# Turned outputs issued piece by piece, the inverse's fourth product one step later, and two sets of key factors put in by ScalarE

## The chip, the cores and the metric

The kernel runs on one core of one Trainium2 chip. The core has five engines with instruction queues of their own: TensorE (PE in the profile, its weight loads PEld), VectorE (DVE), ScalarE (ACT), GpSimd (POOL) and SyncE (SP). SP only issues transfers here; ScalarE's queue issues transfers too, between its arithmetic. The metric is the device time of one execution in microseconds (us), as the median of several runs. The kernel before takes 2236.08 us, the median of three runs from 2230.81 to 2239.41.

## What is computed

One layer of a decoder: a normalised input (512 tokens of 2048) is projected once, and the columns of the projection feed two causal token mixers, their gates and two merge gates. The mLSTM has 8 heads, the gated DeltaNet 16. Their outputs go through one output projection, are merged with sigmoid gates and added to the input; a last RMSNorm ends it. Cut to what matters here:

```python
u = rmsnorm(x, norm_w)
(ml_q, ml_k, ml_v, ml_o, ml_z, ml_i, ml_f,
 dn_qkv, dn_z, dn_b, dn_a, gate_a, gate_b) = split(u @ w_in)

# mLSTM, per head and chunk
kw = k_c * exp(we_c - m_new)[..., None]
C_new = decay * C + einsum('sd,se->de', kw, v_c)

# gated DeltaNet, per head and chunk
a_mat = where(strict, beta[..., :, None] * (k @ k.T) * decay_mat, 0.0)
sol = triangular_solve(a_mat + eye, rhs, lower=True, unit_diagonal=True)
u_ = w_val - w_k @ S
o = q_dec @ S + qk @ u_
S_new = g_end * S + k_end.T @ u_

y = sigmoid(gate_a) * (h_a @ w_out[:2048]) + sigmoid(gate_b) * (h_b @ w_out[2048:])
out = rmsnorm(x + y) * final_norm_w
```

## The kernel before

**Products in fp32 from two halves.** Each weight tile (wr) is loaded by SP, and then split: ScalarE rounds it to a high part wh (L135), VectorE subtracts to get the low part wl (L138). Three products for each pair of tiles (wh by uh, wh by ul, wl by uh: L261 to L263) give nearly the exact fp32 product. Weights are loaded four blocks ahead (RAHEAD) and split three blocks ahead (SAHEAD).

**The stages.** First the input is normalised, then come the projections that need no channel-major layout, in a Strassen-like scheme of seven products for eight (`seven_stage`, L575 to L577). Then comes the stage of the mixers: eight units (`dn_unit`), one for two DeltaNet heads each, numbered 0 to 7 here. A unit projects its keys, in units 3 to 6 the query and key of one mLSTM head too, then its values and queries (`proj_cm`). After that come the output projection and the end.

**What sets the order.** The order on TensorE is the order of the code. A projection calls `tick()` after every six products: that is a step. All other work of the mixers is written as generators, and each `yield n` hands the engine back for n steps. So the small products of the mixers stand between the projection's products at places that the yields fix. On the other engines a scheduler sets the order, from priorities (`urgent`) and from `behind(eng)`, which places an instruction after the newest split on that engine. An engine then runs its queue strictly in that order, so an instruction that waits holds all behind it.

**The parts around the change:**

- `turn` (L790 to L797) transposes a tile of a head in 32x32 blocks on VectorE. `travel` (L799 to L812) then finishes the transpose through DRAM, with four transfers (L806) of 64 KB each. Keys, values and queries go by SP's queue, to a buffer td and back (L811). Outputs go by ScalarE's queue to h_d (DeltaNet) or hm_d (mLSTM) and are read only in the output projection. An output's `travel` starts `lag` steps after its transpose: five, and three for the heads of the last unit.
- `dn_front_k` (L814) makes the triangular matrix of a unit. The products of keys by keys (pk, L841) are taken with the decay into aq (L843), the factors cs (beta over the squared norm) are put in at L857, and the diagonal 32x32 blocks go to DRAM (ld, L860) and come back as ls (L870), one system to a partition. After `yield 10` VectorE solves them by forward substitution (tmp at L881, xi at L883).
- `dn_back` (L923) puts the inverse together from the blocks by four sets of small products: p1 (L937), p2 (L948), p3 (L959) and p4 (L966). Between them ScalarE and VectorE move results from PSUM: s1 (L942), tb (L955), s3 (L962), tb again (L968). Two steps lie between p3 and p4. Then the chains of the two heads (`dn_chain`, L976) run over the four chunks: pr (L990), r (L993), pw (L998), w (L1001), pst (L1005), the state st (L1009, L1011).
- `ml_head` does an mLSTM head: the keys kw are multiplied by the factors we on VectorE (L1110), the chunks follow at L1117 to L1135, and the two halves of the output are turned at L1156.
- `conv_silu` (L766) takes a projection from PSUM with ScalarE (yp, L770); the next projection's second tile in PSUM waits for that.

Of the kernel before, what the change touches and what calls it, by code (L numbers as in the profile page):

```python
# [11 lines left out]
ALU = mybir.AluOpType  # L12
# [3 lines left out]
P = 128  # L16
S = 512
NC = S // P
# [24 lines left out]
BS = 32  # L43
# [12 lines left out]
def hybrid_body(  # L56
# [16 lines left out]
    nc = tc.nc  # L73
    ctx.enter_context(tc.manual_schedule(engines={mybir.EngineType.PE}))
    V, A, G, T = nc.vector, nc.scalar, nc.gpsimd, nc.tensor
# [64 lines left out]
    def behind(eng):  # L140

        return tc.issue_after(newest[eng])
# [66 lines left out]
    def urgent(level=1):  # L209
        return tc.high_priority(offset=level * PRIO)  # L210
# [6 lines left out]
    def start(gen, wait=0, by=None):  # L217
        active.append([gen, clock["t"] + wait, held["by"] if by is None else by])
# [544 lines left out]
    def bc(col, n):  # L763
        return col.unsqueeze(2).to_broadcast([P, NC, n])
# [11 lines left out]
    def silu_end(dst, then=None):  # L776
        th = wkb.tile([P, S], F32, tag="th", name="th", bufs=2)
        with behind("A"):
            A.activation(th, dst, AF.Tanh)
        V.scalar_tensor_tensor(out=dst, in0=th, scalar=1.0, in1=dst, op0=ALU.add, op1=ALU.mult)  # L780
        if then is not None:
            turn(*then)
        yield 1
# [8 lines left out]
    def turn(src, dst, out=False, lag=5):  # L792


        o = dst if dst is not src and len(dst.shape) == 3 else wk.tile([P, NC, P], F32, tag="to", name="to", bufs=2)
        V.transpose(o if len(src.shape) == 3 else o.rearrange("p n c -> p (n c)"), src)
        start(travel(o, dst, out), lag if out else 2)  # L797

    def travel(o, dst, out):  # L799

        d = dst if len(dst.shape) == 4 else dr.tile([16, BS, 4, BS], F32, tag="td", name="td", bufs=8)
        ov = o.rearrange("p n (j c) -> p (n j) c", c=BS)
        q = nc.scalar if out else nc.sync
        with behind("A") if out else urgent(2):
            for a in range(4):
                q.dma_start(d[:, :, a, :].rearrange("m r c -> r m c"), ov[a * BS:(a + 1) * BS])  # L806
        if d is dst:
            return
        yield 4
        with behind("A") if out else urgent(2):  # L810
            q.dma_start(dst, d.rearrange("(n j) r a c -> (j r) n (a c)", n=NC))  # L811
        yield 1  # L812

    def dn_front_k(hs, kq, u):  # L814
# [18 lines left out]
        cs = wk.tile([P, 2, NC], F32, tag="cs", name="cs")  # L833

        for j in range(2):
            aq = u["pool"].tile([P, NC, 2, P], F32, tag="aq", name="aq", bufs=2)
# [15 lines left out]
            V.tensor_tensor(out=cs[:, j, :], in0=cs[:, j, :], in1=beta[:, :, hs[j]], op=ALU.mult)  # L852
        u["nk"] = nk
        ld = dr.tile([2 * NC, 4, BS, BS], F32, tag="ld", name="ld", bufs=2)
        for j in range(2):
            aq = u["aq"][j]
            V.tensor_tensor(out=aq[:, :, 0, :], in0=aq[:, :, 0, :], in1=bc(cs[:, j, :], P), op=ALU.mult)  # L857
            for b in range(4):
                bs = slice(b * BS, (b + 1) * BS)
                nc.sync.dma_start(ld[j * NC:(j + 1) * NC, b, :, :].rearrange("c s t -> s c t"), aq[bs, :, 0, bs])  # L860
# [11 lines left out]
        G.memset(xi, 0.0)  # L872
        for q in range(4):
            G.memset(xi.rearrange("p m t -> p (m t)")[q * NSYS:(q + 1) * NSYS, q:(BS // 4) * BS:BS + 4], 1.0)
        yield 10
        for i in range(BS - 1):
            n, m = BS - 1 - i, i // 4 + 1
            tmp = wkb.tile([P, 80], F32, tag="tmp", name="tmp")
            tv = tmp[:, 0:n * m].rearrange("p (a b) -> p a b", b=n)
            with behind("V"):  # L880
                V.tensor_tensor(out=tv, in0=ls[:, i, i + 1:BS].unsqueeze(1).to_broadcast([P, m, n]),  # L881
                                in1=xi[:, 0:m, i].unsqueeze(2).to_broadcast([P, m, n]), op=ALU.mult)
# [40 lines left out]
    def dn_back(hs, kq, u):  # L923

        tn, tt = u["tn"], u["tt"]
        G2 = [(j * NC + c, u["aq"][j][:, c, 0, :]) for j in range(2) for c in range(NC)]
        for b in range(4):
            bs = slice(b * BS, (b + 1) * BS)
            G.tensor_copy(tb[bs, :, bs], tt[bs])
        for b in range(2):  # L930
            bs = slice(b * BS, (b + 1) * BS)
            G.tensor_copy(ta[bs, :, bs], tn[bs])
        p1 = psw.tile([P, 2 * NC, BS], F32, tag="wk", name="p1")
        for g, a in G2:
            for q in range(2):
                a0, a1 = slice(64 * q, 64 * q + 32), slice(64 * q + 32, 64 * q + 64)
                T.matmul(p1[a1, g, :], a[a0, a1], tn[a0, g, :], start=True, stop=True)  # L937
        s1 = wk.tile([P, 2 * NC, BS], F32, tag="s3", name="s1", bufs=1)
        for q in range(2):
            a1 = slice(64 * q + 32, 64 * q + 64)  # L940
            with urgent():
                A.mul(s1[a1], p1[a1], -1.0)  # L942
        yield 2
        p2 = psw.tile([P, 2, 2 * NC, BS], F32, tag="wk", name="p2")
        for g, a in G2:
            for q in range(2):
                a0, a1 = slice(64 * q, 64 * q + 32), slice(64 * q + 32, 64 * q + 64)
                T.matmul(p2[a0, 0, g, :], s1[a1, g, :], tt[a1, g, :], start=True, stop=True)  # L948
            T.matmul(p2[32:64, 1, g, :], tt[32:64, g, :], s1[32:64, g, :], start=True, stop=True)
        with urgent(2):  # L950
            V.tensor_copy(ta[32:64, :, 0:32], p2[32:64, 1])
        for q in range(2):
            a0, a1 = slice(64 * q, 64 * q + 32), slice(64 * q + 32, 64 * q + 64)
            with urgent():
                A.copy(tb[a0, :, a1], p2[a0, 0])  # L955
        yield 3
        p3 = psw.tile([P, 2 * NC, 64], F32, tag="wk", name="p3")
        for g, a in G2:
            T.matmul(p3[64:128, g, :], a[0:64, 64:128], ta[:, g, :], start=True, stop=True)  # L959
        s3 = wk.tile([P, 2 * NC, 64], F32, tag="s3", name="s3", bufs=1)  # L960
        with urgent():
            A.mul(s3[64:128], p3[64:128], -1.0)  # L962
        yield 2
        p4 = psw.tile([P, 2 * NC, 64], F32, tag="wk", name="p4")
        for g, a in G2:
            T.matmul(p4[0:64, g, :], s3[64:128, g, :], tb[64:128, g, 64:128], start=True, stop=True)  # L966
        with urgent():
            V.tensor_copy(tb[0:64, :, 64:128], p4[0:64])  # L968
        for j in range(2):
            vn = u["vs"][j]  # L970
            with behind("V"):
                V.tensor_tensor(out=vn, in0=vn, in1=bc(u["nk"][:, j, :], P), op=ALU.mult)
        start(dn_chain(0, hs, kq, u), 2)
        start(dn_chain(1, hs, kq, u), 3)

    def dn_chain(j, hs, kq, u):  # L976
# [54 lines left out]
        with urgent():  # L1031
            V.tensor_tensor(out=g, in0=po, in1=g, op=ALU.mult)
        turn(g, h_d[h], True, 5 if h < 2 * UNITS[-1][0] else 3)

    def dn_unit(p, mh):
# [7 lines left out]
        for j in range(2):  # L1043
            ke = u["pool"].tile([P, NC, P], F32, tag="ke", name="ke", bufs=2)
            u["ke"].append(ke)
            conv_silu(ps[j], 16 + hs[j], kq[j][:, 0, :])
            start(silu_end(kq[j][:, 0, :], (kq[j][:, 0, :], ke)), 4 + 3 * j, front)
        start(dn_front_k(hs, kq, u), 1, front)
        if mh is not None:
            ps = proj_cm(mh, kind="m")  # L1050
            mkq = wkb.tile([P, 2, S], F32, tag="mkq", name="mkq", bufs=1)
            with urgent():
                A.mul(mkq[:, 1, :], ps[0], float(P) ** -0.5)
            with urgent():
                A.copy(mkq[:, 0, :], ps[1])
            start(ml_head(mh, mkq), 1, "B")
# [10 lines left out]
        for j in range(2):  # L1067
# [3 lines left out]
            start(silu_end(kq[j][:, 1, :], (kq[j][:, 1, :], qn)), 4 + 3 * j, front)  # L1071
        start(dn_front_q(hs, kq, u), QWAIT + 3 * last, by)
        start(dn_back(hs, kq, u), (25 if mh is None else 9) + 4 * last, by)

    def ml_head(h, kq):
        kT, qT = kq[:, 0, :], kq[:, 1, :]
        kw = wkb.tile([P, NC, P], F32, tag="mkw", name="kw", bufs=1)
        with behind("V"):
            turn(kT, kw)
# [11 lines left out]
        we = wk.tile([P, NC], F32, tag="we", name="we")  # L1091
# [14 lines left out]
        G.memset(v1[:, :, NB:NB + 1], 1.0)  # L1106
        nc.sync.dma_start(v1[:, :, 0:NB], v_d[:, :, h * NB:(h + 1) * NB].rearrange("c p n -> p c n"))
        yield 6
        with behind("V"):
            V.tensor_tensor(out=kw, in0=kw, in1=bc(we, P), op=ALU.mult)  # L1110
        yield 2

        sq = wk.tile([P, NC], F32, tag="sq", name="sq")
# [39 lines left out]
        for i in range(2):  # L1153
            with behind("V"):
                V.tensor_tensor(out=g[i], in0=v1[:, :, i * P:(i + 1) * P], in1=g[i], op=ALU.mult)
            turn(g[i], hm_d[2 * h + i], True)  # L1156
            yield 1

    def ml_first(h):

        kq = wkb.tile([P, 2, S], F32, tag="mkq", name="mkq", bufs=1)
        for i in range(2):
            nc.sync.dma_start(kq[:, 1 - i, :], qk_d[2 * QKFIRST * i + h])
        yield 4
        yield from ml_head(h, kq)
# [481 lines left out]
```

## Time and profile before

| what | before |
|---|---|
| median of three runs | 2236.08 us |
| profiled execution, its own time | 2233.9 us |
| its span, first to last instruction | 2232.1 us |
| mean granted clock of TensorE | 0.994 |
| stage of the mixers, in the span | about 1081 to 1880 us |
| VectorE, ScalarE and GpSimd busy in that stage | 590.7, 360.7 and 199.3 of 799.0 us |

The profile is of one execution on the chip. "PE p L966 <- ACT s L962: 7.8, 4, 2.6" among the waits says that TensorE's product at line 966 waited for ScalarE's instruction at line 962, 7.8 us in total, four times, 2.6 at most. In the timeline a row has its start, its length, engine, line and operation, and in brackets the idle time of the engine before it and what ended that. A row of the windows has the stretch, its length, the busy time of PE, PEld, DVE, ACT and POOL with the number of instructions, then the granted clock of TensorE as a share of the full one, the share of the DMA engines and GB/s. ACTq and SPq are the queues that issue transfers; issuing isn't counted as busy.

### The profile page before, as it was taken

Reading aid. Unit: us, or ns where it says so; the run is one execution under the profiler, and the core shown is the slowest. Engines: PE = TensorE matmul, PEld = TensorE weight load, DVE = VectorE, ACT = ScalarE, POOL = GpSimd, SP = SyncE. Lnnn points to the kernel's source line nnn. Section 1 sums busy time; section 2 is a strip of 40 time slices with the busy share of each in tenths; the row PEclk is TensorE's granted clock in tenths of the full one; section 3 lists DMA queues with packets and bytes.
Section 4 is the critical chain, followed back from the end, with each engine's and each line's share of the span. In section 5 each row is a group of like instructions: output and inputs, shape, how many; then the busy total and the mean of one; then the engine's idle time right before and its main releaser. Section 6 shows DMA issues by size and latency. Waiting matters only on the chain. (4 is left out here: it accounts for less than half of the span.)

```text
span 2232.1 us, 31548 instructions
## 1 busy us (share of the span) xinstructions
PE 2159.3 (97%) x10592; PEld 1771.9 (79%) x10592; DVE 1671.0 (75%) x2907; ACT 995.0 (45%) x1890; POOL 276.6 (12%) x356
## 2 busy tenths in 40 slices
PE   7999999999999999999999999999999999999997
PEld 5877878888788788788878887878888887877775
DVE  5787788888878777877588876757675868667875
ACT  5444444444444343444544544444444445344344
POOL 0320000000000000000222422222222211110101
PEclk9999999999999999999999999999999999999999
DMA  5456666667667766776776767676756568695896
GB/s 156 125 174 193 199 201 201 205 202 231 197 208 228 235 210 205 229 244 192 195 189 168 179 145 174 147 172 166 178 139 167 141 153 230 186 278 184 250 317 215
DMA packets 534821, 435.81 MB, mean 195 GB/s; under 512 B 241921, under 2 KB 393698, under 8 KB 534530
## 3 DMA queue, kind: packets, MB, share of 16 engines
q1 hardware_dynamic: 425058, 357.68, 56.4%
q10 hardware_dynamic: 105568, 68.77, 9.8%
q0 software_dynamic: 4032, 7.34, 2.2%
q8 instruction: 83, 1.36, 0.3%
q14 instruction: 80, 0.66, 0.1%
HBM read 342.37 MB, written 95.49 MB: 196 GB/s over the span
## 5 line engine op out<-in xcount | busy, mean ns | idle before, releaser
L135 ACT CAST wh<-wr 128x512 fp32r<-128x512 f32 (+1 forms) x538 | 379.9, 707 | 470.9 <-PE pj L262 261.8
L138 DVE TENSOR_TENSOR wl<-wr,wh 128x512 fp32r<-128x512 f32 (+1 forms) x538 | 447.2, 834 | 178.2 <-ACT wh L135 160.2
L261 PE MATMUL pj<-uh,wh 128*128 128x512 f32 x1024 | 431.6, 421 | 4.2 <-ACT yp L770 4.2
L263 PE MATMUL pj<-uh,wl 128*128 128x512 f32 x1024 | 404.3, 395 | 0.0
L262 PE MATMUL pj<-ul,wh 128*128 128x512 f32 x1024 | 403.2, 394 | 0.0
L576 PE MATMUL ps<-wl,uh 128*128 128x512 f32 x704 | 277.3, 394 | 7.2 <-DVE wl L138 7.0
L575 PE MATMUL ps<-wh,uh 128*128 128x512 f32 x704 | 276.3, 392 | 7.0 <-DVE X L617 6.5
L577 PE MATMUL ps<-wh,ul 128*128 128x512 f32 x704 | 275.0, 391 | 0.0
L135 ACT CAST wh<-ts 128x512 fp32r<-128x512 f32 x224 | 138.2, 617 | 256.3 <-DVE ts L535 192.2
L135 ACT CAST wh<-t 128x1024 fp32r<-128x1024 f32 x112 | 117.9, 1053 | 250.9 <-PE ps L577 122.8
L263 PEld LDWEIGHTS pj<-uh,wl 128*128 128x128 f32 x1024 | 194.1, 190 | 43.3
L261 PEld LDWEIGHTS pj<-uh,wh 128*128 128x128 f32 x1024 | 195.2, 191 | 40.8 <-ACT yp L770 5.4
L576 PE MATMUL ps<-wl,suh 128*128 128x512 f32 x576 | 224.2, 389 | 1.6 <-DVE wl L138 1.6
L575 PE MATMUL ps<-wh,suh 128*128 128x512 f32 x576 | 224.5, 390 | 0.8 <-ACT qk L353 0.3
L577 PE MATMUL ps<-wh,sul 128*128 128x512 f32 x576 | 224.1, 389 | 0.0
L262 PEld LDWEIGHTS pj<-ul,wh 128*128 128x128 f32 x1024 | 195.6, 191 | 33.4
L138 DVE TENSOR_TENSOR wl<-ts,wh 128x512 fp32r<-128x512 f32 x224 | 153.6, 689 | 38.0 <-ACT wh L135 38.0
L138 DVE TENSOR_TENSOR wl<-t,wh 128x1024 fp32r<-128x1024 f32 x112 | 137.6, 1229 | 48.0 <-ACT wh L135 47.4
L576 PEld LDWEIGHTS ps<-wl,uh 128*128 128x128 f32 x704 | 132.6, 188 | 43.1 <-DVE wl L138 16.7
L575 PEld LDWEIGHTS ps<-wh,uh 128*128 128x128 f32 x704 | 132.5, 188 | 40.5 <-DVE X L617 12.7
L577 PEld LDWEIGHTS ps<-wh,ul 128*128 128x128 f32 x704 | 132.5, 188 | 26.7
L535 DVE TENSOR_TENSOR ts<-wr 128x512 f32<-128x512 f32 x112 | 77.2, 690 | 99.8 <-DMA wr<-t_d 76.0
(302 smaller groups left out, 3462.5 us busy)
## 6 DMA issues: line engine op xcount, KB each, us to landing
wr<-in_w_in_dram SPq DMA_DIRECT2D x704, 256.0 KB, 3.7
wr<-in_w_out_dram SPq DMA_DIRECT2D x138, 256.0 KB, 4.8
t_d<-ts ACTq DMA_DIRECT2D x96, 256.0 KB, 4.4
wr<-t_d SPq DMA_DIRECT2D x96, 256.0 KB, 4.1
wr<-in_w_in_dram SPq DMA_DIRECT2D x64, 128.0 KB, 3.2
xt<-in_x_dram SPq DMA_DIRECT2D x8, 512.0 KB, 7.2
tg_d<-X ACTq DMA_DIRECT2D x16, 256.0 KB, 6.1
tg_d<-to ACTq DMA_DIRECT2D x16, 256.0 KB, 5.1
```

The source lines that it names most:

```text
L135: newest["A"] = A.copy(hi, src).ins
L138: newest["V"] = V.tensor_tensor(out=lo, in0=src, in1=hi.bitcast(F32), op=ALU.subtract).ins
L261: T.matmul(ps[j], hi[:, k, wsl], uh[:, kt, :], start=(kt == 0), stop=False)
L262: T.matmul(ps[j], hi[:, k, wsl], ul[:, kt, :], start=False, stop=False)
L263: T.matmul(ps[j], lo[:, k, wsl], uh[:, kt, :], start=False, stop=(kt == KT - 1))
L535: V.tensor_tensor(out=ts[:, 0, :], in0=r[:, 0, :], in1=r[:, 2, :], op=ALU.subtract)
L575: T.matmul(ps[t], ah, hi, start=(g == "A" and i == 0), stop=False, skip_group_check=True)
L576: T.matmul(ps[t], ah, lo, start=False, stop=False, skip_group_check=True)
L577: T.matmul(ps[t], al, hi, start=False, stop=(i == KH - 1), skip_group_check=True)
```

## The change

There are four edits, all in the stage of the mixers. The four transfers of an output that is turned with a lag of five steps are issued one by one, a step apart, instead of together, each placed behind the newest split on ScalarE; in an mLSTM head the second half's turn comes three steps later, so that the two don't overlap. The factors cs are put into aq by eight ScalarE multiplies of 128x128 for a unit instead of two of 128x512 on VectorE, three steps later; each head's diagonal blocks are sent a step after its multiplies, and seven steps instead of ten lie between the last of it and the substitution. The factors we are put into kw by four ScalarE multiplies instead of one on VectorE. And p4 comes three steps after p3, not two, with the chains behind it.

```diff
-        start(travel(o, dst, out), lag if out else 2)
+        start(travel(o, dst, out, lag > 3), lag if out else 2)
 
-    def travel(o, dst, out):
+    def travel(o, dst, out, apart):
...
-        q = nc.scalar if out else nc.sync
-        with behind("A") if out else urgent(2):
+        if out:
             for a in range(4):
-                q.dma_start(d[:, :, a, :].rearrange("m r c -> r m c"), ov[a * BS:(a + 1) * BS])
-        if d is dst:
+                with behind("A"):
+                    nc.scalar.dma_start(d[:, :, a, :].rearrange("m r c -> r m c"), ov[a * BS:(a + 1) * BS])
+                if apart:
+                    yield 1
             return
...
     def dn_front_k(hs, kq, u):
...
+        yield 3
         for j in range(2):
             aq = u["aq"][j]
-            V.tensor_tensor(out=aq[:, :, 0, :], in0=aq[:, :, 0, :], in1=bc(cs[:, j, :], P), op=ALU.mult)
+            with behind("A"):
+                for c in range(NC):
+                    A.mul(aq[:, c, 0, :], aq[:, c, 0, :], cs[:, j, c:c + 1])
+            yield 1
...
-        yield 10
+        yield 7
         for i in range(BS - 1):
...
     def dn_back(hs, kq, u):
...
             A.mul(s3[64:128], p3[64:128], -1.0)
-        yield 2
+        yield 3
         p4 = psw.tile([P, 2 * NC, 64], F32, tag="wk", name="p4")
...
     def ml_head(h, kq):
...
-        with behind("V"):
-            V.tensor_tensor(out=kw, in0=kw, in1=bc(we, P), op=ALU.mult)
+        with behind("A"):
+            for c in range(NC):
+                A.mul(kw[:, c, :], kw[:, c, :], we[:, c:c + 1])
...
             turn(g[i], hm_d[2 * h + i], True)
-            yield 1
+            yield 4
```

How the queues move: in unit 4, in ScalarE's queue between the evictions of p1 and of p3, before:

```order
L942 ACTIVATE s_14692<-p_14675 32x256 x2
L135 CAST wh<-wr 128x512
L806 DMA hm_d<-to 32x16x32 x4
L955 COPY tb<-p_14727 32x8x32 x2
L135 CAST wh<-wr 128x512
L806 DMA hm_d<-to 32x16x32 x3
L135 CAST wh<-wr 128x512
L806 DMA hm_d<-to 32x16x32
L962 ACTIVATE s_14798<-p_14789 64x512
```

and after:

```order
L950 ACTIVATE s_14737<-p_14720 32x256 x2
L135 CAST wh<-wr 128x512
L806 DMA hm_d<-to 32x16x32
L963 COPY tb<-p_14775 32x8x32 x2
L135 CAST wh<-wr 128x512
L806 DMA hm_d<-to 32x16x32 x2
L135 CAST wh<-wr 128x512
L806 DMA hm_d<-to 32x16x32 x2
L970 ACTIVATE s_14840<-p_14831 64x512
```

The issues of the turned output (hm_d, from the transposed tile "to") between the two evictions go from eight to five, two at most together. On SP, in the same unit, the writes of the diagonal blocks (ld) and their reading back (ls), among loads of weights (wr), before:

```order
L860 DMA ld<-aq 32x4x32 x4
L176 DMA wr<-in_w_in_dram 128x2x256
L860 DMA ld<-aq 32x4x32 x4
L176 DMA wr<-in_w_in_dram 128x2x256
L870 DMA ls<-ld 32x1024 x4
```

and after:

```order
L868 DMA ld<-aq 32x4x32 x7
L176 DMA wr<-in_w_in_dram 128x2x256
L868 DMA ld<-aq 32x4x32
L878 DMA ls<-ld 32x1024 x2
L176 DMA wr<-in_w_in_dram 128x2x256
L878 DMA ls<-ld 32x1024
L812 DMA td<-kw 32x16x32 x4
L878 DMA ls<-ld 32x1024
```

The last read now stands behind a weight load more and the four writes of an mLSTM key (td). The place of unit 0's last projection on ScalarE, where the first head's output goes out, before:

```order
L135 CAST wh<-wr 128x512 x4
L806 DMA hm_d<-to 32x16x32 x3
L770 COPY yp_9097<-pj 128x512
L806 DMA hm_d<-to 32x16x32
L135 CAST wh<-wr 128x512
```

and after:

```order
L135 CAST wh<-wr 128x512 x4
L806 DMA hm_d<-to 32x16x32
L770 COPY yp_9097<-pj 128x512
L771 ACTIVATE kq_9106<-yp_9097,convc 128x512
L135 CAST wh<-wr 128x512
L806 DMA hm_d<-to 32x16x32
```

One issue stands ahead of the projection's first eviction (yp) where three stood.

More of the change, by code (lines that the diff above doesn't have):

```diff
@@ L796, in turn @@
         V.transpose(o if len(src.shape) == 3 else o.rearrange("p n c -> p (n c)"), src)
-        start(travel(o, dst, out), lag if out else 2)
-    def travel(o, dst, out):
+        start(travel(o, dst, out, lag > 3), lag if out else 2)
+    def travel(o, dst, out, apart):
         d = dst if len(dst.shape) == 4 else dr.tile([16, BS, 4, BS], F32, tag="td", name="td", bufs=8)
         ov = o.rearrange("p n (j c) -> p (n j) c", c=BS)
-        q = nc.scalar if out else nc.sync
-        with behind("A") if out else urgent(2):
+        if out:
             for a in range(4):
-                q.dma_start(d[:, :, a, :].rearrange("m r c -> r m c"), ov[a * BS:(a + 1) * BS])
-        if d is dst:
+                with behind("A"):
+                    nc.scalar.dma_start(d[:, :, a, :].rearrange("m r c -> r m c"), ov[a * BS:(a + 1) * BS])
+                if apart:
+                    yield 1
             return
+        with urgent(2):
+            for a in range(4):
+                nc.sync.dma_start(d[:, :, a, :].rearrange("m r c -> r m c"), ov[a * BS:(a + 1) * BS])
         yield 4
-        with behind("A") if out else urgent(2):
-            q.dma_start(dst, d.rearrange("(n j) r a c -> (j r) n (a c)", n=NC))
+        with urgent(2):
+            nc.sync.dma_start(dst, d.rearrange("(n j) r a c -> (j r) n (a c)", n=NC))
         yield 1
```

## The prediction

> **What bounds the kernel now.** I read the page first, then the waits of TensorE, then ScalarE in the stretch where TensorE waits, and last the granted clock. The page gives the span and the busy shares:
>
> ```profile
> span 2232.1 us, 31548 instructions
> PE 2159.3 (97%) x10592; PEld 1771.9 (79%) x10592; DVE 1671.0 (75%) x2907; ACT 995.0 (45%) x1890; POOL 276.6 (12%) x356
> ```
>
> TensorE is busy for all but 72.8 us, so the change can only win back idle time or clock. It touches only the stage of the two mixers, from about 1081 us to 1880 us. The waits of TensorE in that window (total, times, longest), and the table of windows for the stage and for some short stretches in it:
>
> ```profile
> PE p L966 <- ACT s L962: 7.8, 4, 2.6
> PE pj L261 <- ACT yp L770: 4.2, 3, 2.1
> PE pr L990 <- DVE st L1009: 2.4, 1, 2.4
> PE py L1306 <- ACT yp L770: 2.3, 2, 1.7
> PE pw L998 <- DVE tb L968: 1.4, 1, 1.4
> PE pk L841 <- DVE kq L780: 0.4, 1, 0.4
> PE pst L1005 <- DVE st L1011: 0.4, 1, 0.4
> ...
> 1081.00:1880.00 799.00, 780.02 (x4428) 649.71 (x4427) 590.72 (x1433) 360.74 (x911) 199.29 (x252) 0.99 0.69 166
> ...
> 1140.00:1143.00 3.00, 3.00 (x9) 2.32 (x8) 2.62 (x7) 2.86 (x6) 0.00 (x0) 0.50 1.10 156
> 1389.20:1392.50 3.30, 3.30 (x12) 2.72 (x11) 3.02 (x14) 0.00 (x0) 0.00 (x0) 0.50 0.43 100
> 1464.20:1467.60 3.40, 1.53 (x18) 1.42 (x19) 2.08 (x4) 2.71 (x5) 0.89 (x1) 1.00 1.17 308
> 1467.70:1471.00 3.30, 3.30 (x9) 2.58 (x8) 3.27 (x6) 1.40 (x3) 0.00 (x0) 0.50 0.73 195
> 1689.50:1692.90 3.40, 3.40 (x9) 2.63 (x8) 3.37 (x5) 1.40 (x3) 0.77 (x1) 0.50 0.77 195
> 1802.20:1805.50 3.30, 3.30 (x9) 2.55 (x9) 3.27 (x6) 1.22 (x3) 0.00 (x0) 0.50 0.44 129
> ```
>
> The waits sum to 18.9 us, which is the stage's whole idle time (799.0 - 780.0 = 19.0). The largest is p4 (L966) waiting for ScalarE's eviction of p3. Behind five of these waits the clock column reads 0.50 for some 3.4 us, so each costs about another 1.7 us; the stage's mean of 0.99 says the same (1% of 799 is 8 us, five times 1.7 is 8.5). Idle and clock together hold 27.4 us: no more can be gained in this stage.
>
> Why is the eviction late? ScalarE's timeline ahead of the worst case, and TensorE there:
>
> ```profile
> 1455.62 4.44 ACTq L806 DMA_DIRECT2D hm_d<-to  x4
> 1460.11 0.36 ACT L955 COPY tb<-p 32x256 f32<-32x256 f32 x1 [7.37 <-DMA td<-qn]
> 1460.32 0.40 ACTq L806 DMA_DIRECT2D hm_d<-to  x1
> 1460.48 0.36 ACT L955 COPY tb<-p 32x256 f32<-32x256 f32 x1
> 1460.87 0.62 ACT L135 CAST wh<-wr 128x512 fp32r<-128x512 f32 x1
> 1463.13 0.93 ACTq L806 DMA_DIRECT2D hm_d<-to  x2
> 1464.18 0.62 ACT L135 CAST wh<-wr 128x512 fp32r<-128x512 f32 x1 [2.69 <-PE pj L263]
> 1465.01 0.31 ACTq L806 DMA_DIRECT2D hm_d<-to  x1
> 1465.42 0.59 ACT L962 ACTIVATE s<-p 64x512 f32<-64x512 f32 x1 [0.63 <-DMA wr<-in_w_in_dram]
> ...
> 1466.07 0.33 PE L966 MATMUL p<-tb,s 64*64 64x64 f32 x2 [2.59 <-ACT s L962]
> ...
> L806 ACTq DMA_DIRECT2D hm_d<-to x64: 309/310/737, 1132.3 to 1798.7; - x64
> ```
>
> The four pieces of one turned output hold ScalarE's queue for 4.44 us, though one issue takes 0.31 us (4 x 0.31 = 1.24): between them the queue waits for earlier transfers. Eight such issues stand in front of this eviction, and ScalarE sits idle for 7.37 us behind the first ones. ScalarE is not short of time; it is blocked.
>
> **The change part by part.** One step (tick) is six products. Two rows on TensorE that lie three products apart give the length:
>
> ```profile
> 1455.89 0.40 PE L261 MATMUL pj<-uh,wh 128*128 128x512 f32 x1
> ...
> 1456.58 0.39 PE L261 MATMUL pj<-uh,wh 128*128 128x512 f32 x1
> ```
>
> That is 0.69 us for three, so 1.38 us for a step. *p4 one step later, pieces apart.* The order of ScalarE's queue in unit 4 (heads 8 and 9), shown with the change, has between the evictions of p1 and p3 five pieces instead of eight, and never more than two together. At 4.44 / 4 = 1.11 us a piece the eviction comes 3.3 us sooner, at about 1462.7 instead of 1466.0, and p4, which could have started at 1463.5, is asked for 1.38 us later, at 1464.9. The wait goes: -7.8 us. From below: the later step alone takes at most 4 x 1.38 = 5.5. Three of the half-clock stretches (1467.7, 1689.5, 1802.2) follow these waits: -5.1.
>
> The rule of the Trainium skill, "TensorE: Matmul & The Clock Gate", Part 1, What's actually happening, is that a whole idle window of about 3.4 us brings half the clock back. Here 1.87 us idle in a 3.40 us window (1464.2 row) was enough, so the row decides; by the rule this term would be 0.
>
> *First evictions of a projection (L770).* 4.2 + 2.3 us are lost to them, with one half-clock stretch (1140). The longest, 2.1, has three pieces of the first head ahead of it; the changed order of unit 0, shown with the change, leaves one: -2.1 and -1.7. The rest, 4.4, lies where the DeltaNet outputs go out, and there three pieces still stand ahead of the eviction in seven units. I take half, -2.2 (bounds 0 and -4.4). The wait for tb (1.4) comes from a split that was late behind pieces: half, -0.7.
>
> *Products moved to ScalarE.* The rows of what goes (VectorE, aq and kw) and the nearest row of what comes (a 128x128 activation with a per-partition operand):
>
> ```profile
> L857 DVE TENSOR_TENSOR aq<-aq,cs x16: 683/689/693, 1103.7 to 1824.8; 128x512 f32<-128x512 f32 x16
> L1110 DVE TENSOR_TENSOR kw<-kw,we x8: 682/684/685, 1091.8 to 1747.1; 128x512 f32<-128x512 f32 x8
> L828 ACT ACTIVATE dm<-dm,ngam x64: 385/387/393, 1094.4 to 1816.4; 128x128 f32<-128x128 f32 x64
> ```
>
> VectorE loses 24 x 0.69 = 16.5 us, ScalarE gains 96 x 0.387 = 37.2, which takes it from 45% to 50% of the stage. Neither is TensorE's time while evictions are on schedule. A burst of eight is 3.1 us; in units 0 to 2 one stands between the tb copies and the eviction of p3, where no wait was before and the extra step gives 1.38. I take +1 (bounds 0 and 3 x 1.7).
>
> *A shorter head start for the substitution.* ld (the diagonal blocks) used to be written ten steps before the substitution reads it back as ls (13.8 us); now the second half of it can be written seven to eight steps before (9.7 to 11.0 us). Issue on SP (minimum, median, maximum ns) and time to landing:
>
> ```profile
> L860 SPq DMA_DIRECT2D ld<-aq x64: 302/430/1707, 1104.4 to 1828.9; - x64
> L870 SPq DMA_DIRECT2D ls<-ld x32: 307/412/615, 1110.7 to 1832.6; - x32
> ...
> ls<-ld SPq DMA_DIRECT2D x32, 128.0 KB, 3.6
> ...
> ld<-aq SPq DMA_DIRECT2D x64, 16.0 KB, 2.0
> ...
> 1386.47 0.19 DVE L881 TENSOR_TENSOR tmp<-ls,xi 128x31 f32<-128x31 f32 x1 [6.99 <-DMA ls<-ld]
> ```
>
> Eight issues, a landing, four issues and a landing are 3.4 + 2.0 + 1.6 + 3.6 = 10.7 us, before any weight load between them. The margin falls from 3.1 us to about nothing. On SP, as its order in unit 4 shows, the last ls has moved behind another weight load and the four writes of a key. So VectorE will wait at the first tmp more often; queued behind it are the splits (L138) and, in units 1 to 3, the state copies of the preceding unit's chains. Before, it waited twice (6.99 here), and once TensorE followed, for 2.4 us and a half clock: that is the lowest price of one, 4.1. I keep it and add one more: +4 (bounds 0 and three more, 12.3).
>
> *The rest* (turned outputs landing up to three steps later, the two output buffers held as much longer, the chains and the tail one step later) I take at nothing: no reader of h_d or hm_d comes soon, and TensorE has 97% of the span as cover.
>
> **Sum:** -7.8 - 5.1 - 2.1 - 1.7 - 2.2 - 0.7 + 1 + 4 = -14.6 us. Against the profiled execution's own 2233.9 us that is 2219.3; the median of the runs shown, 2236.1, lies 2.2 higher, so 2221.5.
>
> **The rivals.** *All of it comes back:* no new wait, and every wait of the stage and its half clocks go, up to -27.4: 2209 to 2216. For it: one cause, the pieces, stands behind most of them. Against it: the state copy at L1009 has another cause.
>
> *The waits move to ScalarE:* the bursts delay evictions as the pieces did. If half of their 37.2 us is exposed, the 19.6 of gains are nearly eaten (-1): 2227 to 2241 with the ls waits in part. For it: ScalarE's queue is in order and the first evictions keep three pieces ahead. Against it: ScalarE idles half the stage. A rule of the Trainium skill speaks for this one ("ScalarE: Activation LUTs", Rules for kernel authors): plain multiplies belong on VectorE, not on ScalarE. By the rows above the moved work is 2.3 times as long.
>
> *The half clocks stay,* since they come from the windows' phase and not from these waits: then 6.8 of the gains fall away, and 2228.3 is left. Against it: each of the five follows a wait. This is what the clock rule cited above would make of it.
>
> *Slower:* the short head start decides. If VectorE waits for ls 4.1 us longer (three steps) and TensorE follows by that much, one unit costs 2.4 + 4.1 + 1.7 = 8.2; four units (1 to 3 and 7) are 33 us, less 19.6 of gains: +13, 2249. It decides from four units on. Against it: in units 4 to 6 the chain's reads now stand ahead of the first tmp, and splits are made three blocks ahead.
>
> **How the numbers follow.** About 0.5% (11 us) is what a measurement of this kernel can tell from no change. Forecast 0.48 (2216 to 2227, of which 0.38 lies below 2225), all of it 0.12, moved to ScalarE 0.25, half clocks stay 0.05, slower 0.10. So faster 0.38 + 0.12 = 0.50, same 0.10 + 0.25 + 0.05 = 0.40, slower 0.10. The range 2208 to 2241 leaves out the slower case and the edges of the others. The forecast's own range is 2216 to 2227.
>
> **What would show it.** Right: the row of p4 waiting for s is gone or under 2 us in total, the pieces are issued singly with little idle time on ScalarE behind them, and at most two windows of 0.50 are left in the stage. Wrong: a row of TensorE waiting for st, r or pw behind tmp with more than 5 us, waits on L770 above 5 us, or half clocks without a wait ahead of them.

## The result, and the profile after

| what | before | after |
|---|---|---|
| median | 2234.53 us (14 runs, 2224.55 to 2239.41) | 2226.58 us (14 runs, 2220.53 to 2233.40) |
| ratio of the times | 1 | 0.9966, 95% interval 0.9954 to 0.9977 |
| profiled execution | 2233.9 us, span 2232.1 | 2228.3 us, span 2226.5 |
| mean granted clock | 0.994 | 0.994 |

The change makes the kernel faster by 0.34%: 8.0 us by the medians, where the sum had 14.6. The page of after:

```profile
span 2226.5 us, 31649 instructions
...
PE 2157.8 (97%) x10592; PEld 1770.6 (80%) x10592; DVE 1650.0 (74%) x2883; ACT 1022.2 (46%) x1986; POOL 265.2 (12%) x356
```

VectorE has 21 us less than before, ScalarE 27 us more, and TensorE has lost little of its idle time: 68.7 us of the span are left, of 72.8. The waits of TensorE in the stage of the mixers, 1081 to 1880 us:

```profile
PE p L974 <- ACT s L970: 4.3, 3, 1.9
PE pw L1006 <- DVE tb L976: 4.2, 3, 1.9
PE py L1315 <- ACT yp L770: 2.2, 2, 1.8
PE pnum L1128 <- DVE c L1138: 1.8, 1, 1.8
PE pr L998 <- DVE st L1017: 0.9, 1, 0.9
...
```

The windows of the same stage and of its half clocks:

```profile
1081.00:1880.00 799.00, 785.48 (x4468) 655.52 (x4468) 577.97 (x1442) 390.94 (x1011) 189.11 (x252) 0.99 0.69 169
1457.00:1460.20 3.20, 3.20 (x16) 2.70 (x16) 2.40 (x4) 2.45 (x5) 0.00 (x0) 0.50 1.02 239
1460.40:1463.50 3.10, 3.10 (x9) 2.42 (x8) 3.07 (x5) 2.14 (x9) 0.00 (x0) 0.50 0.47 102
1576.40:1579.60 3.20, 3.20 (x10) 2.55 (x9) 3.20 (x6) 2.51 (x11) 0.00 (x0) 0.50 0.31 82
```

Lines have moved by eight or nine: p4 is L974 now, the eviction of p3 L970. The stage's idle time falls from 18.9 to 13.6 us, and five half-clock stretches become three (two of them behind one wait). That is 5.3 + 2 x 1.7 = 8.7 us, about the gain of the medians, though these are one execution each and the 14 of a kernel spread over 13 to 15 us. The two profiled executions differ by 5.6 us only: outside the stage the one of after has 1.2 us more idle time (55.1 against 53.9; its py waits 4.7 us for wh in the output projection, before's 2.4), and half clocks in other places, so that the mean granted clock is 0.994 in both.

In the stage, first evictions of the key and query projections (pj waiting for yp, 4.2) have left the list. The wait of p4 is halved and not gone, and a wait of pw for tb, 1.4 before, stands at 4.2.

Why p4 still waits is in ScalarE's timeline ahead of the worst case, the same place as in the prediction:

```profile
1440.40 0.78 ACT L950 ACTIVATE s<-p 32x256 f32<-32x256 f32 x2 [2.48 <-PE p L945]
...
1443.95 0.35 ACTq L806 DMA_DIRECT2D hm_d<-to  x1
...
1446.61 3.25 ACTq L806 DMA_DIRECT2D hm_d<-to  x2
1450.03 0.62 ACT L135 CAST wh<-wr 128x512 fp32r<-128x512 f32 x1 [3.11 <-DMA hm_d<-to]
1453.85 1.86 ACTq L806 DMA_DIRECT2D hm_d<-to  x2
1455.81 0.59 ACT L970 ACTIVATE s<-p 64x512 f32<-64x512 f32 x1 [5.16 <-DMA hm_d<-to]
```

Five pieces stand between the evictions now, as the order said, but the two that are issued together at 1446.61 hold the queue for 3.25 us, and the eviction of p3 has 5.16 us of idle time ahead of it. From the end of p1's eviction (1440.40 + 0.78 = 1441.18) to the start of p3's it takes 14.6 us. In before it took 13.9 (from 1451.47 to 1465.42), with eight pieces between. Fewer pieces did not bring it nearer. ScalarE's waits for transfers of outputs, over the whole span, sum to 29.5 us after:

```profile
ACT s L970 <- DMA hm_d<-to: 14.0, 3, 5.2
...
ACT wh L135 <- DMA hm_d<-to: 9.3, 3, 3.1
...
ACT wh L135 <- DMA h_d<-to: 6.2, 1, 6.2
```

The largest rows of this kind before:

```profile
ACT tb L955 <- DMA td<-qn: 13.3, 2, 7.4
ACT tb L955 <- DMA hm_d<-to: 12.5, 2, 6.5
```

Before, the rows of outputs sum to 30.0 us (12.5, 7.5, 5.7 and 4.3), and rows of SP's writes to td add 16.2, the 7.37 us that the prediction shows among them. So the change shortens the waits that are put down to td and leaves those for outputs as long as they were; 14.0 us of them now lie directly ahead of the eviction of p3.

Why pw waits is in the timelines of the next unit. On TensorE, its p4 and its first pw:

```profile
1569.60 1.14 PE L974 MATMUL p<-tb,s 64*64 64x64 f32 x16 [1.39 <-ACT s L970]
...
1575.60 0.49 PE L1006 MATMUL pw<-vt,tb 128*128 128x128 f32 x2 [1.91 <-DVE tb L976]
```

On VectorE between the two:

```profile
1570.94 0.75 DVE L773 SCALAR_TENSOR_TENSOR kq<-yp,convc,kq 128x512 f32<-128x512 f32 x1 [5.93 <-ACT kq L771]
...
1573.42 1.41 DVE L773 SCALAR_TENSOR_TENSOR kq<-yp,convc,kq 128x512 f32<-128x512 f32 x2
1574.86 0.68 DVE L976 COPY tb<-p 64x512 f32<-64x512 f32 x1
```

p4 ends at 1570.74, and its copy to tb starts 4.1 us later. In VectorE's order it stands behind three operations of the next projection's convolution (L773), where before only one stood ahead of it, while pw comes as many steps after p4 as it did. The step that p4 got has put its copy further back. VectorE itself had been idle for 5.93 us before the first of the three, waiting for ScalarE (kq, L771). These waits grow with the pieces apart: 13.8 us over the span before, 39.3 after, 34.3 in the kernel below with the pieces apart alone.

The new multiply of aq on ScalarE:

```profile
L864 ACT ACTIVATE aq<-aq,cs x64: 384/387/400, 1104.4 to 1817.5; 128x128 f32<-128x128 f32 x64
```

387 ns is the estimate to the ns; the 32 of kw have a median of 390. VectorE's wait for ls over the whole span, before and after, and the first tmp of the unit whose wait was 6.99 us before:

```profile
DVE tmp L881 <- DMA ls<-ld: 11.1, 2, 7.0
...
DVE tmp L889 <- DMA ls<-ld: 0.7, 2, 0.5
...
1379.35 0.19 DVE L889 TENSOR_TENSOR tmp<-ls,xi 128x31 f32<-128x31 f32 x1 [4.17 <-DMA kw<-td]
```

The wait put down to ls falls from 11.1 us to 0.7, where I had expected more of it. It is not all gone: 4.17 us of idle time ahead of a first tmp are put down to another transfer (kw from td), so that VectorE is idle for 4.9 us there in place of 11.1.

### The profile page after: what moved, and what is told of

Same layout as the page of the kernel before. It is cut to its first block, busy times and chain, and to the rows that moved or that the text cites. A ratio compares the mean times of both kernels' runs of the same rounds, so it can differ in the third digit from the quotient of the medians.

```text
span 2226.5 us, 31649 instructions
## 1 busy us (share of the span) xinstructions
PE 2157.8 (97%) x10592; PEld 1770.6 (80%) x10592; DVE 1650.0 (74%) x2883; ACT 1022.2 (46%) x1986; POOL 265.2 (12%) x356
## 5 line engine op out<-in xcount | busy, mean ns | idle before, releaser
L138 DVE TENSOR_TENSOR wl<-wr,wh 128x512 fp32r<-128x512 f32 (+1 forms) x538 | 440.9, 822 | 152.9 <-ACT wh L135 142.7
L576 PEld LDWEIGHTS ps<-wl,uh 128*128 128x128 f32 x704 | 132.3, 188 | 43.6 <-DVE wl L138 17.3
```

The source lines that it names most:

```text
L138: newest["V"] = V.tensor_tensor(out=lo, in0=src, in1=hi.bitcast(F32), op=ALU.subtract).ins
L576: T.matmul(ps[t], ah, lo, start=False, stop=False, skip_group_check=True)
```

## The experiments

The theory after the result: what costs is that ScalarE's queue, which runs in order, is held by the pieces of turned outputs while each waits for an earlier transfer; spreading the pieces helps the first evictions of a projection, the later step only hands p4's wait on to pw, and the multiplies on ScalarE are neutral. The first rival: the later step is what gains. The second: the engines' loads decide, so that moving the multiplies does it. Each run below is timed against the kernel before on the same chip; medians and ratios are of several runs, the waits of one profiled execution. The profiled execution is not always a typical one. It was the slowest execution of its kernel, so that its waits are probably more than the usual ones, with the pieces apart alone (2238.91 us), aq alone (2238.45), the chains later (2235.69), aq back on VectorE (2233.41), SyncE (2223.26) and GpSimd without the step (2213.59). It was the fastest with the whole change without the step (2219.86) and with GpSimd and the step (2209.96).

**The pieces apart, alone.** The kernel before with this edit:

```diff
             turn(g[i], hm_d[2 * h + i], True)
-            yield 1
+            yield 4
...
+                with behind("A"):
+                    nc.scalar.dma_start(d[:, :, a, :]..., ov[a * BS:(a + 1) * BS])
+                if apart:
+                    yield 1
```

> The kernel before with one edit alone: an output's four transfers a step apart, and the second half of an mLSTM output three steps later. Theory (a piece waits for an earlier transfer to land, and that wait is not shorter when pieces are spread): p4's wait for s stays at 6 to 8 us, since p4 keeps its step; only the waits for yp shrink, from 4.2 + 2.3 us to 3 or less; time 2 to 4 us below before. Rival (the prediction's: a piece costs 1.11 us of queue, and fewer stand ahead): p4's wait falls by 5 us or more and half clocks with it; 8 us or more below before.

Measured: 2226.91 us against 2237.48, ratio 0.9964 (0.9949 to 0.9980). The waits of TensorE in the stage, and one of ScalarE:

```profile
PE p L970 <- ACT s L966: 9.3, 5, 3.3
...
PE py L1310 <- ACT yp L770: 3.9, 2, 3.6
PE pj L261 <- ACT yp L770: 0.2, 1, 0.2
...
ACT s L966 <- DMA hm_d<-to: 10.1, 2, 5.3
```

This edit alone has the whole gain of the change (0.9966). p4's wait is no smaller for it, and ScalarE still stands in front of p3's eviction until a transfer to hm_d lands. What went is the wait of pj for yp, from 4.2 to 0.2; py's stands at 3.9 (2.3 before), so yp costs 4.1 us and not 3 or less, and the gain is larger than the 2 to 4 us expected. pj's wait is gone or at 0.2 in every kernel with the pieces apart or out of ScalarE's queue, and at 4.0 to 5.9 in the three others. That this is where the gain comes from isn't shown by this execution, one as slow as those of before, with 17.3 us of waits in the stage against 18.9.

**The later step, alone.** `yield 2` to `yield 3` between p3 and p4, and nothing else.

> The kernel before with p4 three steps after p3, nothing else. Theory (p4 asked for later, but its result then queues on VectorE behind the next projection's convolutions): p4's wait for s falls from 7.8 to 4 us or less, pw's wait for tb rises from 1.4 to 3 to 5 us, the waits for yp stay; time 0 to 3 us below before. Rival (the prediction's step alone): p4's wait falls to 2.3, pw's stays at 1.4, half clocks go: 6 to 9 us below.

Measured: 2237.41 us against 2237.48, ratio 1.0001 (0.9988 to 1.0014).

```profile
PE pw L998 <- DVE tb L968: 7.8, 5, 2.3
...
PE p L966 <- ACT s L962: 2.2, 2, 1.4
```

p4's 7.8 us fall to 2.2, and pw's 1.4 rise to 7.8. The sum of the two is 9.2 before and 10.0 here. The step is worth nothing, and the wait is passed on whole.

**The multiplies, alone.** In one kernel the factors of aq on ScalarE with the steps of the substitution that belong to it, in another the factors of kw:

```diff
-            V.tensor_tensor(out=aq[:, :, 0, :], in0=aq[:, :, 0, :], in1=bc(cs[:, j, :], P), op=ALU.mult)
+            with behind("A"):
+                for c in range(NC):
+                    A.mul(aq[:, c, 0, :], aq[:, c, 0, :], cs[:, j, c:c + 1])
...
-        with behind("V"):
-            V.tensor_tensor(out=kw, in0=kw, in1=bc(we, P), op=ALU.mult)
+        with behind("A"):
+            for c in range(NC):
+                A.mul(kw[:, c, :], kw[:, c, :], we[:, c:c + 1])
```

> The kernel before with cs put into aq by ScalarE, with the new steps around it (3, 1, 1, 7 for 10). Theory (from the changed kernel's trace): VectorE's wait for ls falls from 11.1 us to under 2, TensorE's wait of 2.4 for the state goes with its half clock: 3 to 5 us below before. Rival 1 (the prediction's term): ls comes later relative to the substitution, VectorE waits 11 us or more and TensorE follows once more: 4 us above. Rival 2 (bursts delay evictions): p4's and yp's waits grow by 3 us or more.

> The kernel before with we put into kw by ScalarE, nothing else. Theory: 8 bursts of 4 multiplies of 0.39 us stand where nothing on TensorE waits; within 1.5 us of before. Rival (ScalarE is the late engine): waits for yp, s or w grow, 3 us or more above.

Measured: aq 2234.34 us, ratio 0.9980 (0.9967 to 0.9994); kw 2231.85 us, ratio 0.9974 (0.9963 to 0.9985). Neither costs anything, and each gains a little by itself, kw more than the 1.5 us expected at most. Why isn't shown: with kw alone p4 still waits 7.0 us and pj 5.8. In the execution with aq alone TensorE still waits as before, and VectorE's wait for ls is there, four times:

```profile
PE p L970 <- ACT s L966: 7.5, 4, 4.1
...
DVE tmp L885 <- DMA ls<-ld: 11.5, 4, 6.2
```

The wait for ls hasn't gone under 2 us, as expected from the changed kernel's trace. Whether the short head start lengthens it can't be told: it is 11.5 us in four places here, 11.1 in two before, 7.1 to 14.0 in the other kernels with the old head start and 0.7 to 12.5 in those with the new one. TensorE follows the longest of these waits (6.2): pr waits 3.0 us for the state copy right behind it, and a half clock comes after that, as before (2.4 us). The Trainium skill ("ScalarE: Activation LUTs", Rules for kernel authors) has plain multiplies on VectorE and not on ScalarE. Both ratios speak against that here, though the moved work is 2.3 times as long. ScalarE is busy for 45% of the time and VectorE for 75%, which may be why; no run tests it.

By the ratios, of some 2236 us, the four parts alone gain 8.0, -0.2, 4.5 and 5.8 us. They sum to 18, and the change gains 7.6: the parts don't add up.

**The whole change without the later step,** p4 two steps after p3 as before:

> The changed kernel with p4 two steps after p3, as before: pieces, aq and kw without the later step. Theory (the step only hands p4's wait on to pw, so it is worth nothing here either): p4's wait for s 6 us or more, pw's for tb under 2, time as the changed kernel, 5 to 11 us below before. Rival 1 (the parts add up: 8.0, 4.5 and 5.8 were measured alone): 16 to 20 us below. Rival 2 (the step is needed once ScalarE has the multiplies): less than 4 us below.

Measured: 2229.33 us against 2234.68, ratio 0.9973 (0.9958 to 0.9988), which is the change's own within the intervals. p4's wait is 8.3 us and pw waits for tb no more:

```profile
PE p L974 <- ACT s L970: 8.3, 3, 3.5
```

Again the two waits exchange places (4.3 + 4.2 with the step, 8.3 without).

**The chains a step later too,** so that pw keeps its distance from p4's copy:

```diff
-        start(dn_chain(0, hs, kq, u), 2)
-        start(dn_chain(1, hs, kq, u), 3)
+        start(dn_chain(0, hs, kq, u), 3)
+        start(dn_chain(1, hs, kq, u), 4)
```

> The changed kernel with both chains one step later, so that three steps lie between p4 and the first pw too. Theory (pw waits only since tb's copy stands behind the next projection's convolutions): pw's wait for tb falls from 4.2 us to under 1, nothing takes its place, 3 to 6 us below the changed kernel, 11 to 14 below before. Rival (a wait is handed on once more, to r or the state): pr, pst or pw wait for r or st by 3 us or more, time as the changed kernel, 8 below before.

Measured: 2231.26 us against 2234.68, ratio 0.9978 (0.9967 to 0.9988). The wait of pw for tb is gone, but the 11 to 14 us expected did not come, and the time is no better than the change's: in the profiled execution p4 waits 8.0 us, three times. Moving readers later does not remove a late eviction.

**The pieces issued by GpSimd.** In the changed kernel the four transfers of an output go to a queue with no evictions in it; then the same with p4 two steps after p3:

```diff
-                with behind("A"):
-                    nc.scalar.dma_start(d[:, :, a, :]..., ov[a * BS:(a + 1) * BS])
+                nc.gpsimd.dma_start(d[:, :, a, :]..., ov[a * BS:(a + 1) * BS])
```

> The changed kernel with the turned outputs issued from GpSimd's queue, not ScalarE's. Theory (ScalarE is held by the pieces, which wait for earlier transfers): p4's wait for s under 1.5 us, yp's under 1, ScalarE's waits for hm_d and h_d gone (29 us now); pw's for tb stays at 3 to 5: 12 to 16 us below before. Rival (GpSimd's queue is held instead, and VectorE and TensorE wait for it): waits of DVE or PE for POOL instructions of 5 us or more, 8 us below before at best.

> As the run with GpSimd's queue, but p4 two steps after p3. Theory (without pieces on ScalarE the later step has nothing to cure): p4's wait under 2 us, pw's for tb under 2: 14 to 20 us below before. Rival (ScalarE's evictions and multiplies alone make s late): p4's wait 4 us or more, no better than with the step.

Measured: 2216.51 us, ratio 0.9911 (0.9896 to 0.9926), and without the step 2210.55 us, ratio 0.9888 (0.9874 to 0.9902), both against 2234.68. They gain 18 and 24 us by the medians, more than the 12 to 16 and 14 to 20 expected; with the step, pw waits 1.1 us and not 3 to 5, and yp costs 2.3 and not under 1. The second is the fastest kernel of this study, and the later step does not help it either. Its waits of TensorE in the stage:

```profile
PE py L1314 <- ACT yp L770: 3.4, 2, 2.6
PE pr L997 <- DVE st L1016: 1.2, 1, 1.2
...
PE pw L1005 <- DVE tb L975: 0.6, 1, 0.6
```

Its window of the stage:

```profile
1081.00:1880.00 799.00, 793.17 (x4545) 662.12 (x4544) 591.14 (x1449) 397.10 (x1033) 288.06 (x377) 1.00 0.67 172
```

Its issues (minimum, median, maximum ns):

```profile
L805 POOL DMA_DIRECT2D hm_d<-to x64: 648/651/900, 1128.6 to 1771.3; - x64
```

ScalarE from p1's eviction to p3's in unit 4:

```profile
1438.23 0.78 ACT L949 ACTIVATE s<-p 32x256 f32<-32x256 f32 x2 [2.49 <-PE p L944]
...
1446.85 0.62 ACT L135 CAST wh<-wr 128x512 fp32r<-128x512 f32 x1 [2.10 <-PE pj L262]
1448.16 0.59 ACT L969 ACTIVATE s<-p 64x512 f32<-64x512 f32 x1 [0.70 <-PE p L966]
```

The list has no row of p4, the stage is idle for 5.8 us instead of 13.6, and its granted clock rounds to 1.00. p3's eviction comes 9.2 us after the end of p1's (14.6 in the changed kernel), and what it waits for is now TensorE's p3 itself. An issue takes GpSimd 651 ns where it took ScalarE 310, and nobody waits for GpSimd the longer for it: VectorE's waits for it sum to 15.6 us over the span, 23.0 in the changed kernel, and TensorE has none in the stage.

**Only the queue.** The kernel before, with its four transfers still together, issued by GpSimd; nothing else of the change:

```diff
-        q = nc.scalar if out else nc.sync
-        with behind("A") if out else urgent(2):
+        q = nc.gpsimd if out else nc.sync
+        with urgent(0) if out else urgent(2):
```

> The kernel before with one edit: the four transfers of a turned output are issued by GpSimd instead of ScalarE, still four together, and p4, aq and kw are as before. Theory (what costs is ScalarE's in-order queue held by these transfers): most of the gain of the version with GpSimd's queue comes from this alone, ratio 0.988 to 0.994, with p4's wait for s under 2 us and the first evictions' wait (yp) under 3 us in the stage of the mixers. Rival (the gain needs the pieces apart and the multiplies on ScalarE as well): ratio 0.995 to 0.999.

Measured: 2219.19 us against 2235.38, ratio 0.9929 (0.9916 to 0.9943), twice what the whole change gains. The complete list of TensorE's waits in the stage:

```profile
PE pr L990 <- DVE st L1009: 6.8, 2, 4.7
PE py L1306 <- ACT yp L770: 3.6, 2, 2.8
```

p4 waits no more, without a later step, without pieces apart, and with aq and kw on VectorE. What is left is py's wait for yp (3.6, where under 3 was expected) and the state copy, which has another cause. 4.7 us of it lie right behind VectorE's longest wait for ls:

```profile
1378.85 0.19 DVE L881 TENSOR_TENSOR tmp<-ls,xi 128x31 f32<-128x31 f32 x1 [9.32 <-DMA ls<-ld]
```

Against 0.9888 for the version above, whose interval lies wholly below this one, pieces, multiplies and substitution steps are worth something beside it.

**aq back on VectorE.** The changed kernel with that one multiply returned:

> The changed kernel with the multiply of aq back on VectorE, its steps kept as in the change. Theory (ScalarE's multiplies are neutral within the change, its queue being held by transfers): ratio to the kernel before 0.9955 to 0.998, as the change itself (0.9966). Rival 1 (the gain that this edit had alone, 4.5 us, is part of the change's gain): 0.998 to 1.000. Rival 2 (eight multiplies in ScalarE's queue delay the evictions): 0.992 to 0.995, with p4's wait for s under 2 us.

Measured: 2227.84 us against 2235.38, ratio 0.9961 (0.9946 to 0.9975). This is the change's own ratio, 0.9966: inside the change, this part gives nothing. p4's wait is 3.5 us in three places and pw's 5.9 in four, against 4.3 in three and 4.2 in three with the multiplies on ScalarE, so these did not delay the evictions either.

**The pieces issued by SyncE.** The 2210.55 us version with `nc.sync` for `nc.gpsimd`: the transfers wait in line with the loads of weights, but no longer ahead of evictions.

> The version with GpSimd's queue and p4 two steps after p3, but the pieces of a turned output issued by SyncE (SP), whose queue also holds all loads of weights; ScalarE issues none of them, and the transfers themselves are the same as in the changed kernel. Theory (the price is that evictions stand behind the transfers in ScalarE's queue): it keeps most of the gain of GpSimd's queue, ratio 0.986 to 0.993, with no p4 wait for s over 1 us and no wait of ScalarE for a transfer to hm_d. Rival (the gain is that GpSimd's transfers do not stand in line with SP's and ScalarE's hardware transfers, whichever engine issues them): SP is held instead, TensorE and ScalarE wait for weights or for ls, ratio 0.995 to 1.005.

Measured: 2216.24 us against 2234.46, ratio 0.9918 (0.9896 to 0.9939), so most of the gain stays. TensorE's waits in the stage, and what ScalarE still waits for:

```profile
PE pr L997 <- DVE st L1016: 4.2, 2, 3.3
PE py L1314 <- ACT yp L770: 2.7, 2, 2.2
PE pw L1005 <- DVE r L1000: 1.8, 2, 1.1
...
ACT wh L135 <- DMA h_d<-to: 4.7, 1, 4.7
ACT wh L135 <- DMA hm_d<-to: 4.2, 2, 2.1
```

No row of p4 again. One detail of the theory fails: ScalarE still stands behind transfers of outputs for 8.9 us (29.5 in the changed kernel, as 14.0 + 9.3 + 6.2), though it issues none of them. What holds it there was not tried. The rival, that only GpSimd's separate kind of transfer helps, is out: it is the engine whose queue is held that matters. The Trainium skill ("DMA: Bandwidth & Descriptors", Issuing engine by pattern) sends simple stores to SyncE and calls GpSimd's path generally the slower one. The first agrees, as the same kernel with ScalarE's queue is the one without the later step, 0.9973 (0.9958 to 0.9988); the second holds for a single issue (651 against 310 ns) and not for the kernel, where GpSimd's queue is no worse than SyncE's.

## Why the prediction was right and wrong

The direction was right and the size about half: 0.34% faster, where 14.6 of 2236 us, 0.65%, was forecast. None of the three signs of being right came: p4's wait is 4.3 us and not under 2, ScalarE still idles behind the pieces, and three half clocks are left and not two. Nor did one of the signs of being wrong. By its steps:

*The diagnosis held.* "ScalarE is not short of time; it is blocked" is what the queue's experiments show: taking the transfers out of ScalarE's queue removes p4's wait in four kernels, with nothing changed in ScalarE's arithmetic in one of them.

*The step that failed is "At 4.44 / 4 = 1.11 us a piece the eviction comes 3.3 us sooner".* It priced a piece, while what holds the queue is the wait of a piece for an earlier transfer. Five pieces held it as long as eight: 14.6 us from p1's eviction to p3's, two pieces alone 3.25. The program names the waits. In ScalarE's order of the changed kernel, eight successive pieces of an output, with the semaphores that each waits for:

```text
908 L806 DMA hm_d<-to 32x16x32 [waits DMAHW2_49,DVE_49]
912 L806 DMA hm_d<-to 32x16x32 [waits DMAHW7_49]
914 L806 DMA hm_d<-to 32x16x32 [waits DMAHW1_49]
919 L806 DMA hm_d<-to 32x16x32 [waits DMAHW4_49]
920 L806 DMA hm_d<-to 32x16x32 [waits DMAHW5_49,DVE_49]
923 L806 DMA hm_d<-to 32x16x32 [waits DMAHW7_49]
924 L806 DMA hm_d<-to 32x16x32 [waits DMAHW0_49]
926 L806 DMA hm_d<-to 32x16x32 [waits DMAHW4_49]
```

Of the 64 pieces to hm_d, 63 wait for one of eight DMA semaphores, which SP's and ScalarE's transfers take in turn, and so for whatever transfer had it last: 44 for one of SP's, 19 for an earlier piece of an output. GpSimd's transfers have eight of their own. That this sharing is what makes the waits long was read, not tried. With SyncE issuing the pieces they still take the same eight, and p4's wait is gone all the same: what costs is whose queue is held.

*The later step.* The sum let it carry 1.38 us of the wait in the worst case, and at most 5.5 alone. Alone it did take 5.6 us off p4's wait, and none off the time. Its step from p4 "asked for 1.38 us later" had nothing for the copy of p4, which VectorE makes behind the convolution of the next projection and which pw needs. Alone the step gives 1.0001, and in the change it moves 4.2 us from p4 to pw.

*The terms.* p4's wait: -7.8 forecast, -3.5 measured, with +2.8 at pw (forecast -0.7). Half clocks of the stage: -6.8 forecast with the one of the first evictions, -3.4 measured. Evictions of a projection: -4.3 forecast, -4.3 measured (6.5 to 2.2), the term that was right in its sum: pj's wait went whole, py's stayed (2.3 to 2.2). With the pieces alone pj's goes too. aq's burst: +1 forecast, nothing measured (0.9961 without it, 0.9966 with it). The substitution's head start: +4 forecast, nothing measured: TensorE's wait behind it (pr for st) fell from 2.4 to 0.9. That TensorE follows a long wait for ls is right, as the kernels with aq alone and with only the queue moved show (3.0 and 4.7 us). A new wait of 1.8 us (pnum for c) stood in no term. The forecast's sum was too large because its largest term was, by 4.3 us, and because the half clocks and pw's wait hang on the same waits. That it came as near as it did is luck in part: the two costs, 5 us together, that never came stood against gains that never came, and without them the sum would have been -19.6.

*The rivals.* "The waits move to ScalarE" gave a time near the result, 2227 to 2241, by a mechanism that no run shows: taking one set of multiplies out again changes neither the time nor p4's wait by much (3.5 us for 4.3). "The half clocks stay", with 2228.3, was near it too: two of the five went. "All of it comes back" describes what a different edit reaches, 2210.55 us with GpSimd's queue. "Slower" had the wait for ls right as a possibility, and TensorE following it in one unit, but its condition, four units, was not met.

## What to carry to other kernels

When an engine with time to spare is late, look in its queue for what waits there and not for what works there: an issue of 0.31 us can hold an in-order queue for several. Move such transfers to an engine that nobody waits for before spreading them or moving the reader; both of these leave the wait in the queue, and the second hands it to the next reader. A stall that is covered by a later step is gone only if what follows that step has a margin of its own.

## What the runs showed of the hardware

In the stage, the clock's half-speed stretches last 3.41 us or twice that. In each of the thirteen traces they all start on one grid of 3.41 us that runs through the execution. Two windows of this grid in the changed kernel, and what follows the second:

```profile
1453.40:1456.80 3.40, 1.49 (x12) 0.95 (x11) 0.00 (x0) 0.96 (x2) 0.63 (x1) 1.00 0.89 227
1685.50:1688.90 3.40, 1.50 (x7) 0.92 (x5) 3.37 (x7) 2.49 (x10) 0.00 (x0) 1.00 0.82 179
1689.00:1692.20 3.20, 3.20 (x16) 2.71 (x17) 3.20 (x6) 2.65 (x12) 0.00 (x0) 1.00 0.25 66
```

In both TensorE is busy for 1.5 us and idle for 1.9. Behind the first the clock is 0.50 for two stretches (1457.00 and 1460.40 above), behind the second it stays at 1.00. These two lie at the edge of what all the traces show. Of the windows of the grid at full clock, from 60 to about 2205 us, those in which TensorE is idle for 1.91 us or more are all followed by half clock (51 of 51). Of those with 1.6 to 1.9 us of idle time it is 19 of 38, and of the 4893 with less it is 2, one of them the window ahead of 1689.50 before, with 1.25 us. So the idle time within one window of the grid decides, apart from a band below 1.9 us that stays open, and a wait that the grid cuts in two may cost nothing more.

The rule of the Trainium skill ("TensorE: Matmul & The Clock Gate", Part 1, What's actually happening) is that a whole idle window of about 3.4 us brings the half clock. The length of the window agrees (3.41 us); the idle time needed is little more than half of it here. A forecast can count the waits with some certainty, but where the grid will lie, and so which of them will cost another 1.7 us, it cannot know from one trace.
